# Layer 1's feed-forward block: raw weights loaded in halves, one low part moved to VectorE, down weights and saved operands asked for at other places

## The chip, the cores and the metric

The kernel runs on one core of a Trainium2 chip. The core has a matrix engine (TensorE, PE in the rows), a vector engine (VectorE, DVE), a scalar engine (ScalarE, ACT), GpSimd (POOL) and a sync engine (SyncE, SP) that here only issues DMAs. The metric is the device time of one execution in microseconds (us), the median of several.

## The reference

Two transformer layers on 1024 tokens of width 1024. Every layer ends with `x = x + g1 * o`, a normalisation, and a SwiGLU feed-forward block (D_FF is 2816 = 22 x 128):

```python
def _swiglu(h, wg, wu, wd):
    return (jax.nn.silu(h @ wg) * (h @ wu)) @ wd
...
        x = x + g1 * o
        h = _rms(x, norm2_g[i]) * (1.0 + sc2) + sh2
        x = x + g2 * _swiglu(h, ffn_w_gate[i], ffn_w_up[i], ffn_w_down[i])
```

The change touches only layer 1 after its attention: the output projection and the feed-forward block, the last 865 us or so of the span.

## The kernel before

All products are made in two parts: a matrix is split into a high part (ScalarE casts it) and a low part (the matrix less its high part), and each product is three matmuls (`mm3`, L74 to L76: high by high, low by high, high by low). TensorE, ScalarE, VectorE and GpSimd each run their own instructions in the order in which a list scheduler set them in this part of the program; SyncE issues its DMAs in program order, and each waits there until the buffer it fills is free.

**Output projection** (`out_proj1`). For each of two column halves of the tokens, ci = 0 and 1, it runs over 8 row tiles dt of x. One row tile is 24 matmuls of 128x512 (`d_ps`) and an update of x by VectorE (L1264). In between it advances two generators of normalisation steps (`norm1s`): `own` for the half in work, and `side`. own0 normalises half 0 and ends in four calls of `combine`, which form the operands `c_hi` and `c_lo` of the products (GpSimd sums `s_sum`, ScalarE casts, VectorE low parts). own1 normalises half 1 and stores its result in DRAM (`h_d`).

**Gate and up** (`gate_up1`). For each of 22 tiles f of D_FF and each half ci, the four products of h's two halves with the gate and up weights are made by a scheme of seven products in place of eight (Winograd's form of Strassen's), each 12 matmuls of 128x256 into a tile `p_ps`: 84 matmuls for a tile. The weight operands are four 128x512 blocks, b11 and b21 (the first and second half of the gate tile), b12 and b22 (of the up tile), and four sums by GpSimd: t1 = b12 - b11 (L1325), t2 = b22 - t1 (L1326), t3 = b22 - b12 (L1341), t4 = t2 - b21 (L1345). The order of the products is b11, t2, t3, t1, t4, b21, b22. The split of an operand is `parts_of`: ScalarE casts the high part (L1239). For the first five operands ScalarE also copies the high part to PSUM (`pmisc`, L1243), and VectorE subtracts (L1244). For b21 and b22 GpSimd subtracts (also L1244). High and low parts live in a ring of six buffers. The raw weights, `w_raw`, live in four buffers of 512 KB, two for a tile, so the load of tile f+2 waits for the last reader of tile f.

**Down** (`down1`). After every second tile the products of two tiles with the down weights are made: 8 row tiles of 6 matmuls of 128x512, 48 in all, into `d_ps`; the last two pairs of a half come together. `down_weights1` loads the down weights of a tile (256 KB each by GpSimd's queue, L1381), casts them (ScalarE, L1382) and makes the low parts (GpSimd, L1383). The parts lie in the two tiles of `h_out[1]` (`h_hi` for even pairs, `h_lo` for odd pairs).

**Between the halves**, the saved operands of half 1 are loaded from `h_d` (`h_in`, L1429) into the same four raw buffers, and `combine` is called at row tiles 1 and 5 of each of the last two `down1` of half 0 (`amid`).

Of the kernel before, what the change touches and what calls it, by code (L numbers as in the profile page):

```python
# [9 lines left out]
F32 = mybir.dt.float32  # L10
F32R = mybir.dt.float32r
AF = mybir.ActivationFunctionType
ALU = mybir.AluOpType
# [3 lines left out]
P = 128  # L17
D = 1024
KT = D // P
SEQ = 1024  # L20
# [3 lines left out]
GW = 64  # L24
GH = SEQ // GW
HD = 64
DFF = 2816
NF = DFF // P
# [35 lines left out]
def build(tc, io):  # L64
    nc = tc.nc
    V, S, G, TE = nc.vector, nc.scalar, nc.gpsimd, nc.tensor
# [45 lines left out]
    def vec(l, which):  # L112
        return mod[l][:, which * KT:(which + 1) * KT, :]
# [1113 lines left out]
    ph, ph_cm = pools.open("ph1", bufs=2, psum=True)  # L1227
    HT = 256

    def raw_weights(src):  # L1230
        raw = wr.tile([P, KT, P], F32, name="w_raw")
        nc.sync.dma_start(raw, src)
        return raw

    def parts_of(src, eng=V, past=True):


        hi, lo = (ww.tile([P, 4, P], F32R, name=n) for n in ("w_hi", "w_lo"))
        S.copy(hi, src)  # L1239
        first = fl(hi)  # L1240
        if eng is V and past:
            first = ph.tile([P, 512], F32, name="pmisc").rearrange("p (k n) -> p k n", n=P)
            S.copy(first, fl(hi))  # L1243
        eng.tensor_tensor(lo, src, first, ALU.subtract)  # L1244
        return hi, lo

    def out_weights(dt):
        raw = raw_weights(io["w_out1"][dt])
        old = wr.tile([P, SEQ], F32, name="x_old", tag="w_raw")
        nc.sync.dma_start(old, x_d[:, dt])  # L1250
        return [parts_of(raw[:, i:i + 4], past=False) for i in (0, 4)], old

    def out_proj1(ci, ready, own, side=iter(()), then=lambda: None):

        h_hi, h_lo = h_out[ci]
        for dt in reversed(range(KT)):
# [7 lines left out]
            V.scalar_tensor_tensor(x[:, dt, ci * 512:ci * 512 + 512].rearrange("p (c r) -> p c r", r=GH),  # L1264
                                   ps.rearrange("p (c r) -> p c r", r=GH), vec(1, 2)[:, dt, 0:1],
                                   old.rearrange("p (r c) -> p r c", c=GW)[:, :, cols].rearrange("p r c -> p c r"),
                                   ALU.mult, ALU.add)
# [55 lines left out]
    def first_sums(g, u):  # L1323
        t1, t2 = (wk.tile([P, 4, P], F32, name=n, tag="t", bufs=4) for n in ("t1", "t2"))
        G.tensor_tensor(t1, u[:, 0:4], g[:, 0:4], ALU.subtract)  # L1325
        G.tensor_tensor(t2, u[:, 4:8], t1, ALU.subtract)  # L1326
        return t1, t2

    def gate_up1(f, side=iter(()), raws=None):
        g, u = raws[:2] if raws else load_gate_up(f)  # L1330
        b11, b21, b12, b22 = g[:, 0:4], g[:, 4:8], u[:, 0:4], u[:, 4:8]
        t1, t2 = raws[2:] if raws else first_sums(g, u)
# [6 lines left out]
        S.copy(p1, ps)  # L1339
        w = parts_of(t2)  # L1340
        G.tensor_tensor(t3, b22, b12, ALU.subtract)  # L1341
        ps = product7(w, 4)
        V.tensor_tensor(u2, ps, p1, ALU.add)
        w = parts_of(t3)
        G.tensor_tensor(t4, t2, b21, ALU.subtract)  # L1345
        ps = product7(w, 5)
        V.tensor_tensor(u3, ps, u2, ALU.add)  # L1347
        w = parts_of(t1)
        ps = product7(w, 3)
        V.tensor_tensor(av[:, 1], ps, u3, ALU.add)  # L1350
        V.tensor_tensor(u2, ps, u2, ALU.add)
# [7 lines left out]
        V.tensor_tensor(sg, ps, p1, ALU.add)  # L1359
# [46 lines left out]
    c_lo = cc.tile([P, 7, 4, HT], F32R, name="c_lo")  # L1406
    own1 = norm1s(1, V, keep)
    def first_tile():
        g, u = load_gate_up(0)
        return g, u, *first_sums(g, u)  # L1410

    ready = out_proj1(1, ready, own1, own0, then=first_tile)
    advance(own0, 99)
    for ci in range(2):
        acts = {}
        for f in range(NF):
            if f < NF - 1:
                down_weights1(f + 1 if f else 0)
            if f == 0:
                down_weights1(1)  # L1420
            acts[f] = gate_up1(f, own1 if f else iter(()), ready if f + ci == 0 else None)
            if f % 2 == 0 and 2 <= f < NF - 2:
                down1(ci, (f - 2, f - 1), [acts.pop(f - 2), acts.pop(f - 1)], False)

        h_in = []
        for i in range(4 if ci == 0 else 0):
            h_in.append(wr.tile([P, 2, 512], F32, name="h_in", tag="w_raw"))
            for n in range(2):
                nc.sync.dma_start(h_in[i][:, n], h_d[:, i + 4 * n])  # L1429

        def amid(dt):
            if dt % 4 == 1 and h_in:
                h = h_in.pop(0)
                combine(3 - len(h_in), h[:, 0], h[:, 1], tags=("t", "t"))

        for f in (NF - 4, NF - 2):
            down1(ci, (f, f + 1), [acts.pop(f), acts.pop(f + 1)], f == NF - 2, amid)
    pools.close(ph_cm, pp_cm, pd_cm, wk_cm, ww_cm, wr_cm, xp_cm, cc_cm, bg_cms[1], cst_cm)


# [110 lines left out]
```

## Time and profile before

| what | us |
|---|---|
| median of 3 runs | 2966.08 (2962.96 to 2969.83) |
| profiled execution: its own time | 2964.59 |
| its span | 2962.5 |
| TensorE busy in the span | 2820.2 |
| gate/up and down of half 0, in the span | about 2194 to 2592 |
| gate/up and down of half 1 | to 2958.7 |

The span is cut into stretches below, named by their start and end in us from the span's start. In a view by stretches each row gives the stretch, its length, the busy time and count of each engine's instructions (PE, PEld, DVE, ACT, POOL), the mean clock granted to TensorE as a share of full speed, the busy share of the DMA engines, and GB/s. In a timeline a row is start, length, engine, line, operation, tile written and tiles read, and in brackets how long the engine was idle before and what ended that.

### The profile page before, as it was taken

Reading aid. Unit: us, or ns where it says so; the run is one execution under the profiler, and the core shown is the slowest. Engines: PE = TensorE matmul, PEld = TensorE weight load, DVE = VectorE, ACT = ScalarE, POOL = GpSimd, SP = SyncE. Lnnn points to the kernel's source line nnn. Section 1 sums busy time; section 2 is a strip of 40 time slices with the busy share of each in tenths; the row PEclk is TensorE's granted clock in tenths of the full one; section 3 lists DMA queues with packets and bytes.
Section 4 is the critical chain, followed back from the end, with each engine's and each line's share of the span. In section 5 each row is a group of like instructions: output and inputs, shape, how many; then the busy total and the mean of one; then the engine's idle time right before and its main releaser. Section 6 shows DMA issues by size and latency. Waiting matters only on the chain. (4 is left out here: it accounts for less than half of the span.)

```text
span 2962.5 us, 44248 instructions
## 1 busy us (share of the span) xinstructions
PE 2820.2 (95%) x16874; PEld 2361.8 (80%) x16874; DVE 1555.9 (53%) x3084; ACT 1196.2 (40%) x2358; POOL 847.3 (29%) x914
## 2 busy tenths in 40 slices
PE   7989999999999999999989999999988999889999
PEld 5876768888888888888867888777767888788888
DVE  5775553623323333333575241666477766766666
ACT  4345552511121111111253231666356666565563
POOL 1112332000000000000220001655257666677764
PEclk9989999999999999999999999999989999999999
DMA  7236564211011010111134335975443333332331
GB/s 275 89 113 235 211 213 139 64 43 36 29 50 43 29 43 30 42 43 37 50 107 133 104 104 151 206 167 119 156 144 114 104 97 97 111 120 86 104 97 58
DMA packets 132069, 310.58 MB, mean 105 GB/s; under 512 B 11505, under 2 KB 69361, under 8 KB 124817
## 3 DMA queue, kind: packets, MB, share of 16 engines
q1 hardware_dynamic: 116384, 265.72, 28.7%
q0 software_dynamic: 8992, 31.40, 3.3%
q10 hardware_dynamic: 6480, 10.63, 1.0%
q8 instruction: 133, 2.18, 0.3%
q14 instruction: 80, 0.65, 0.1%
HBM read 264.58 MB, written 43.12 MB: 104 GB/s over the span
## 5 line engine op out<-in xcount | busy, mean ns | idle before, releaser
L76 PE MATMUL p_ps<-c_hi,w_lo 128*128 128x256 f32 x1232 | 352.3, 286 | 39.1 <-POOL w_lo L1244 31.6
L74 PE MATMUL p_ps<-c_hi,w_hi 128*128 128x256 f32 x1232 | 350.7, 285 | 22.2 <-DVE u L1347 5.6
L75 PE MATMUL p_ps<-c_lo,w_hi 128*128 128x256 f32 x1232 | 349.4, 284 | 0.0
L810 POOL TENSOR_TENSOR nrm_ss<-nrm_ss,nrm_sq 128x512 f32<-128x512 f32 (+1 forms) x31 | 39.3, 1268 | 1013.3 <-PE d_ps L76 935.7
L775 ACT CAST w_hi<-w_raw 128x1024 fp32r<-128x1024 f32 x106 | 110.2, 1049 | 481.0 <-PE d_ps L75 270.5
L76 PEld LDWEIGHTS p_ps<-c_hi,w_lo 128*128 128x128 f32 x1232 | 239.7, 195 | 45.6 <-POOL w_lo L1244 37.1
L74 PEld LDWEIGHTS p_ps<-c_hi,w_hi 128*128 128x128 f32 x1232 | 239.8, 195 | 25.2 <-DVE u L1347 5.8
L75 PEld LDWEIGHTS p_ps<-c_lo,w_hi 128*128 128x128 f32 x1232 | 239.9, 195 | 0.9
L580 POOL TENSOR_SCALAR pr<-pr,st 128x640 f32<-128x640 f32 (+2 forms) x208 | 156.0, 750 | 267.8 <-DVE st L579 177.2
L878 DVE SCALAR_TENSOR_TENSOR x<-d_ps,mod,x 128x512 f32<-128x512 f32 (+1 forms) x240 | 157.6, 661 | 125.3 <-PE d_ps L76 125.3
L776 DVE TENSOR_TENSOR w_lo<-w_raw,w_hi 128x1024 fp32r<-128x1024 f32 x102 | 124.2, 1224 | 183.1 <-ACT w_hi L775 180.7
L862 DVE TENSOR_TENSOR sg<-sg,u_ps 128x512 f32<-128x512 f32 (+1 forms) x66 | 39.5, 599 | 320.2 <-PE u_ps L76 320.2
L74 PE MATMUL d_ps<-act_hi,w_hi 128*128 128x512 f32 (+1 forms) x528 | 189.5, 360 | 3.4 <-DVE x L878 3.4
L75 PE MATMUL d_ps<-act_lo,w_hi 128*128 128x512 f32 (+1 forms) x528 | 189.4, 359 | 1.3 <-DVE act_lo L864 1.3
L76 PE MATMUL d_ps<-act_hi,w_lo 128*128 128x512 f32 (+1 forms) x528 | 189.5, 359 | 0.0
L75 PE MATMUL u_ps<-o_lo,w_hi 128*128 128x512 f32 (+1 forms) x528 | 188.6, 357 | 0.0
L76 PE MATMUL u_ps<-o_hi,w_lo 128*128 128x512 f32 (+1 forms) x528 | 188.6, 357 | 0.0
L74 PE MATMUL u_ps<-o_hi,w_hi 128*128 128x512 f32 (+1 forms) x528 | 188.6, 357 | 0.0
L76 PE MATMUL g_ps<-o_hi,w_lo 128*128 128x512 f32 (+1 forms) x528 | 188.5, 357 | 0.0
L74 PE MATMUL g_ps<-o_hi,w_hi 128*128 128x512 f32 (+1 forms) x528 | 188.5, 357 | 0.0
L75 PE MATMUL g_ps<-o_lo,w_hi 128*128 128x512 f32 (+1 forms) x528 | 188.5, 357 | 0.0
L574 ACT ACTIVATE pr<-sm,st 128x640 f32<-128x640 f32 (+4 forms) x208 | 162.7, 782 | 31.0 <-POOL sm L563 22.2
(323 smaller groups left out, 7464.5 us busy)
## 6 DMA issues: line engine op xcount, KB each, us to landing
ada_w<-ada_w SPq DMA_DIRECT2D x48, 1024.0 KB, 4.9
w_raw<-w_gate SPq DMA_DIRECT2D x66, 512.0 KB, 3.5
w_raw<-w_up SPq DMA_DIRECT2D x66, 512.0 KB, 3.6
wd_raw<-w_down POOLq DMA_DIRECT2D x88, 256.0 KB, 2.9
k<-k_d SPq DMA_DIRECT2D x28, 640.0 KB, 10.3
w_raw<-w_out SPq DMA_DIRECT2D x32, 512.0 KB, 3.6
w_raw<-w_in SPq DMA_DIRECT2D x24, 512.0 KB, 4.1
w_raw<-w_down SPq DMA_DIRECT2D x22, 512.0 KB, 3.5
```

What stands on the lines that cost most here:

```text
L74: TE.matmul(out, lh, rh, start=first, stop=False)
L75: TE.matmul(out, lh, rl, start=False, stop=False)
L76: TE.matmul(out, ll, rh, start=False, stop=last)
L574: S.activation(self.pr[:, :n], self.sm[:, :n], AF.Exp, bias=st[:, 0:1], scale=-1.0, accum_out=st[:, 1:2])
L580: G.tensor_scalar(self.pr[:, :n], self.pr[:, :n], st[:, 3:4], 0.0, ALU.mult, ALU.add)
L775: S.copy(hi, raw)
L776: eng.tensor_tensor(lo, raw, fl(hi), ALU.subtract)
L810: adder(i).tensor_tensor(ss, ss, sq, ALU.add)
L862: V.tensor_tensor(sg[:, :n], sg[:, :n], u_ps[:, :n], ALU.mult)
L878: V.scalar_tensor_tensor(xs, self.shaped(ps[:, :n]), vec(l, 5)[:, dt, v:v + 1], xs, ALU.mult, ALU.add)
```

## The change

`w_raw` becomes eight buffers of 256 KB. A tile is loaded by four DMAs in the order b11, b12, b22, b21 in place of two. The output projection's weights and its old x come in halves through the same buffers, and the update of x is two instructions for 8 of 16 rows each in place of one. The low part of b21 is made by VectorE, with a copy of its high part to PSUM by ScalarE. `side` is advanced by 3 steps for a row tile in place of 2. `down_weights1(f)` is called after `gate_up1(f)`; before, tile f+1's call came ahead of `gate_up1(f)`. The first of the four pairs of saved operands is loaded into two work tiles (tags `nrm_ss` and `nrm_r`), the other three pairs into six half buffers, and `combine` is called at row tiles 3 and 7 of the first of the last two `down1` and at 1 and 4 of the second. Nothing of the arithmetic changes but which engine makes one subtraction. In the changed file the lines named above stand one to three lines lower (L1239 is L1240, L1244 is L1245, L1325 is L1328, L1381 is L1383, L1383 is L1385).

```diff
-    wr, wr_cm = pools.open("raw1", bufs=4)
+    wr, wr_cm = pools.open("raw1", bufs=8)
...
-    def raw_weights(src):
-        raw = wr.tile([P, KT, P], F32, name="w_raw")
-        nc.sync.dma_start(raw, src)
-        return raw
+    def raw_half(src):
+        raw = wr.tile([P, 512], F32, name="w_raw")
+        dst = raw if len(src.shape) == 2 else raw.rearrange("p (k n) -> p k n", n=P)
+        nc.sync.dma_start(dst, src)
+        return dst
...
     def out_weights(dt):
-        raw = raw_weights(io["w_out1"][dt])
-        old = wr.tile([P, SEQ], F32, name="x_old", tag="w_raw")
-        nc.sync.dma_start(old, x_d[:, dt])
-        return [parts_of(raw[:, i:i + 4], past=False) for i in (0, 4)], old
+        ws = [parts_of(raw_half(io["w_out1"][dt][:, i:i + 4]), past=False) for i in (0, 4)]
+        return ws, [raw_half(x_d[:, dt, i:i + 512]) for i in (0, 512)]
...
-            V.scalar_tensor_tensor(x[:, dt, ci * 512:ci * 512 + 512].rearrange("p (c r) -> p c r", r=GH),
...
+            for i in range(2):
+                rows = slice(8 * i, 8 * i + 8)
+                V.scalar_tensor_tensor(
...
             advance(own, 1)
-            advance(side, 2)
+            advance(side, 3)
...
     def load_gate_up(f):
-        return [raw_weights(io[w][1, f]) for w in ("w_gate", "w_up")]
+
+        return [raw_half(io[w][1, f][:, i:i + 4]) for w, i in (("w_gate", 0), ("w_up", 0), ("w_up", 4), ("w_gate", 4))]
...
-        w = parts_of(b21, G)
+        w = parts_of(b21)
...
         for f in range(NF):
-            if f < NF - 1:
-                down_weights1(f + 1 if f else 0)
-            if f == 0:
-                down_weights1(1)
             acts[f] = gate_up1(f, own1 if f else iter(()), ready if f + ci == 0 else None)
+            down_weights1(f)
             if f % 2 == 0 and 2 <= f < NF - 2:
                 down1(ci, (f - 2, f - 1), [acts.pop(f - 2), acts.pop(f - 1)], False)
 
         h_in = []
         for i in range(4 if ci == 0 else 0):
-            h_in.append(wr.tile([P, 2, 512], F32, name="h_in", tag="w_raw"))
-            for n in range(2):
-                nc.sync.dma_start(h_in[i][:, n], h_d[:, i + 4 * n])
-
-        def amid(dt):
-            if dt % 4 == 1 and h_in:
-                h = h_in.pop(0)
-                combine(3 - len(h_in), h[:, 0], h[:, 1], tags=("t", "t"))
+            if i:
+                h_in.append([raw_half(h_d[:, k]) for k in (i, i + 4)])
+            else:
+                h_in.append([wk.tile([P, 512], F32, name="h_in", tag=t) for t in ("nrm_ss", "nrm_r")])
+                for h, k in zip(h_in[0], (0, 4)):
+                    nc.sync.dma_start(h, h_d[:, k])
+
+        def amid(i):
+            if h_in and i in (3, 7, 9, 12):
+                combine(4 - len(h_in), *h_in.pop(0), tags=("t", "t"))
```

**How the order moves.** GpSimd in the steady part, where a row's names are `w_lo` (a low part written), `w_hi` (its high part) and `w_raw` (a raw block; the numbers tell one buffer's use from another). Before, from the low part of tile 11's b22 to that of tile 12's b22:

```order
L1244 TENSOR_TENSOR w_lo_21198<-w_raw_21058,w_hi_21197 128x512
L1325 TENSOR_TENSOR t1_21464<-w_raw_21462,w_raw_21460 128x512
L1326 TENSOR_TENSOR t2_21465<-w_raw_21462,t1_21464 128x512
L1341 TENSOR_TENSOR t3_21468<-w_raw_21462 128x512
L1345 TENSOR_TENSOR t4_21469<-t2_21465,w_raw_21460 128x512
L1244 TENSOR_TENSOR w_lo_21348<-w_raw_21226,w_hi_21347 128x512
L1244 TENSOR_TENSOR w_lo_21368<-w_raw_21228,w_hi_21367 128x512
```

Changed, the same place in the loop (here from tile 9 to tile 10):

```order
L1245 TENSOR_TENSOR w_lo_20918<-w_raw_20774,w_hi_20917 128x512
L1328 TENSOR_TENSOR t1_21194<-w_raw_21188,w_raw_21186 128x512
L1329 TENSOR_TENSOR t2_21195<-w_raw_21190,t1_21194 128x512
L1343 TENSOR_TENSOR t3_21198<-w_raw_21190,w_raw_21188 128x512
L1347 TENSOR_TENSOR t4_21199<-t2_21195,w_raw_21192 128x512
L1245 TENSOR_TENSOR w_lo_21094<-w_raw_20950,w_hi_21093 128x512
```

The low part of b21 has left GpSimd's list; t1 now reads two blocks (b12, b11) that are not the block (b22, now 20774 and 21190) whose buffer the first row sets free.

SyncE's list between the halves. Before, from tile 21's two loads to tile 0's of the second half:

```order
L1232 DMA w_raw_23004<-w_gate 128x1024
L1232 DMA w_raw_23006<-w_up 128x1024
L1429 DMA h_in_23166<-h_d_18025 128x512 x2
L1429 DMA h_in_23169<-h_d_18025 128x512 x2
L1429 DMA h_in_23172<-h_d_18025 128x512 x2
L1429 DMA h_in_23175<-h_d_18025 128x512 x2
L1232 DMA w_raw_23386<-w_gate 128x1024
```

Changed:

```order
L1233 DMA w_raw_23202<-w_gate 128x512
L1233 DMA w_raw_23204<-w_up 128x512
L1233 DMA w_raw_23206<-w_up 128x512
L1233 DMA w_raw_23208<-w_gate 128x512
L1233 DMA w_raw_23382<-h_d_18025 128x512
L1233 DMA w_raw_23384<-h_d_18025 128x512
L1233 DMA w_raw_23386<-h_d_18025 128x512
L1233 DMA w_raw_23388<-h_d_18025 128x512
L1233 DMA w_raw_23390<-h_d_18025 128x512
L1233 DMA w_raw_23392<-h_d_18025 128x512
L1233 DMA w_raw_23586<-w_gate 128x512
```

Six half loads of the saved operands stand here in place of eight; the other two have moved up into the loads of the first half's earlier tiles.

More of the change, by code (lines that the diff above doesn't have):

```diff
@@ L1263, in out_proj1 @@
             cols = slice(ci * 32, ci * 32 + 32)
-            V.scalar_tensor_tensor(x[:, dt, ci * 512:ci * 512 + 512].rearrange("p (c r) -> p c r", r=GH),
-                                   ps.rearrange("p (c r) -> p c r", r=GH), vec(1, 2)[:, dt, 0:1],
-                                   old.rearrange("p (r c) -> p r c", c=GW)[:, :, cols].rearrange("p r c -> p c r"),
-                                   ALU.mult, ALU.add)
+            for i in range(2):
+                rows = slice(8 * i, 8 * i + 8)
+                V.scalar_tensor_tensor(
+                    x[:, dt, ci * 512:ci * 512 + 512].rearrange("p (c r) -> p c r", r=GH)[:, :, rows],
+                    ps.rearrange("p (c r) -> p c r", r=GH)[:, :, rows], vec(1, 2)[:, dt, 0:1],
+                    old[i].rearrange("p (r c) -> p r c", c=GW)[:, :, cols].rearrange("p r c -> p c r"),
+                    ALU.mult, ALU.add)
             advance(own, 1)
-            advance(side, 2)
+            advance(side, 3)
         return ready
@@ L1320, in load_gate_up, with first_sums @@
     def load_gate_up(f):
-        return [raw_weights(io[w][1, f]) for w in ("w_gate", "w_up")]
-    def first_sums(g, u):
+        return [raw_half(io[w][1, f][:, i:i + 4]) for w, i in (("w_gate", 0), ("w_up", 0), ("w_up", 4), ("w_gate", 4))]
+    def first_sums(b11, b12, b22):
         t1, t2 = (wk.tile([P, 4, P], F32, name=n, tag="t", bufs=4) for n in ("t1", "t2"))
-        G.tensor_tensor(t1, u[:, 0:4], g[:, 0:4], ALU.subtract)
-        G.tensor_tensor(t2, u[:, 4:8], t1, ALU.subtract)
+        G.tensor_tensor(t1, b12, b11, ALU.subtract)
+        G.tensor_tensor(t2, b22, t1, ALU.subtract)
         return t1, t2
     def gate_up1(f, side=iter(()), raws=None):
-        g, u = raws[:2] if raws else load_gate_up(f)
-        b11, b21, b12, b22 = g[:, 0:4], g[:, 4:8], u[:, 0:4], u[:, 4:8]
-        t1, t2 = raws[2:] if raws else first_sums(g, u)
+        b11, b12, b22, b21 = raws[:4] if raws else load_gate_up(f)
+        t1, t2 = raws[4:] if raws else first_sums(b11, b12, b22)
         t3, t4 = (wk.tile([P, 4, P], F32, name=n, tag="t", bufs=4) for n in ("t3", "t4"))
@@ L1408, in first_tile @@
     def first_tile():
-        g, u = load_gate_up(0)
-        return g, u, *first_sums(g, u)
+        raws = load_gate_up(0)
+        return *raws, *first_sums(*raws[:3])
     ready = out_proj1(1, ready, own1, own0, then=first_tile)
```

3 lines of the change are left out of this document (2 added, 1 removed).

## The prediction

> **What bounds the kernel now.** I read first how long each stretch of the feed-forward block takes, from the view by stretches (columns: length, then busy time and count of PE, PEld, DVE, ACT, POOL, granted clock, DMA share, GB/s).
>
> ```profile
> 2190.21:2254.04 63.83, 49.00 (x317) 44.64 (x316) 46.53 (x69) 45.30 (x83) 49.03 (x46) 0.87 0.34 118
> 2254.04:2331.52 77.48, 65.31 (x433) 59.23 (x432) 57.05 (x83) 42.85 (x80) 54.96 (x48) 0.96 0.37 119
> 2331.52:2549.56 218.04, 207.02 (x1465) 191.88 (x1464) 142.09 (x255) 135.54 (x247) 151.46 (x132) 0.98 0.30 96
> 2549.56:2642.88 93.32, 78.67 (x483) 69.46 (x481) 63.94 (x103) 49.70 (x96) 68.45 (x64) 0.95 0.38 126
> 2642.88:2907.12 264.24, 249.94 (x1729) 230.33 (x1728) 173.73 (x304) 158.68 (x289) 182.47 (x159) 0.98 0.30 95
> 2907.12:2958.70 51.58, 51.57 (x349) 46.65 (x347) 32.62 (x56) 19.88 (x38) 16.25 (x13) 1.00 0.14 51
> ```
>
> Then what TensorE needs if nothing stalls it: one tile's 84 products and one down, in the same view cut to their own matmuls.
>
> ```profile
> 2293.89:2303.42 9.53, 9.53 (x84) 9.53 (x84) 2.01 (x5) 0.37 (x1) 1.00 0.19 57
> 2417.49:2428.68 11.19, 11.19 (x48) 8.86 (x48) 5.25 (x7) 0.00 (x0) 1.00 0.20 62
> ```
>
> A pair of tiles and its down thus need 2 x 9.53 + 11.19 = 30.25. Against this the stretches lose: the start (three tiles, one down, and 17 last matmuls of the output projection at some 0.23, an estimate from that stage's rate) 63.83 - 39.8 - 3.9 = 20.1; the next four tiles with two downs, beside which the second half's normalisation runs, 77.48 - 60.5 = 17.0; half 0's steady part (14 tiles, 6 downs) 218.04 - 200.6 = 17.4; the passage between the halves (4 tiles, 144 matmuls of down) 93.32 - 71.7 = 21.6; half 1's steady part (8 pairs) 264.24 - 242.0 = 22.2; the end 51.58 - 51.0 = 0.6. Together 99, and nothing else of the program is touched except the output projection.
>
> The steady loss is one loop between two engines and a queue. TensorE waits there for one thing only (waits in 2642.88 to 2907.12; total us, times, longest):
>
> ```profile
> PE p_ps L76 <- POOL w_lo L1244: 14.3, 10, 2.0
> POOL t L1325 <- DMA w_raw<-w_up: 70.6, 16, 5.7
> ```
>
> and GpSimd's timeline shows why, with SyncE's issues under it:
>
> ```profile
> 2433.84 1.31 POOL L1383 TENSOR_TENSOR h_lo<-wd_raw,h_lo 128x512 fp32r<-128x512 f32 x1
> 2435.45 0.55 POOL L1381 DMA_DIRECT2D wd_raw<-w_down  x1 [0.30 <-POOL h_lo L1383]
> 2436.02 1.31 POOL L1244 TENSOR_TENSOR w_lo<-w_raw,w_hi 128x512 fp32r<-128x512 f32 x1
> 2441.78 1.30 POOL L1325 TENSOR_TENSOR t<-w_raw 128x512 f32<-128x512 f32 x1 [4.45 <-DMA w_raw<-w_up]
> 2443.16 1.29 POOL L1326 TENSOR_TENSOR t<-w_raw,t 128x512 f32<-128x512 f32 x1
> 2444.41 1.30 POOL L1341 TENSOR_TENSOR t<-w_raw 128x512 f32<-128x512 f32 x1
> 2445.67 1.26 POOL L1345 TENSOR_TENSOR t<-t,w_raw 128x512 f32<-128x512 f32 x1
> 2446.90 2.51 POOL L1244 TENSOR_TENSOR w_lo<-w_raw,w_hi 128x512 fp32r<-128x512 f32 x2
> 2454.23 1.30 POOL L1325 TENSOR_TENSOR t<-w_raw 128x512 f32<-128x512 f32 x1 [4.82 <-DMA w_raw<-w_up]
> ...
> 2437.36 0.33 SPq L1232 DMA_DIRECT2D w_raw<-w_up  x1
> 2448.19 0.33 SPq L1232 DMA_DIRECT2D w_raw<-w_gate  x1
> 2449.44 0.33 SPq L1232 DMA_DIRECT2D w_raw<-w_up  x1
> ```
>
> The low part of b22 of tile f (2436.02) ends at 2437.33; at 2437.36 the load of tile f+2's up weights leaves; GpSimd stands 4.45 until it has landed, makes t1 to t4, and only then the low parts of b21 and b22 of tile f+1 (the double row). Its next b22 is done 12.1 later (2449.41 less 2437.33). Where no down lies between, TensorE wants it after 9.53. In the other interval of a pair four down low parts with their four issues stand in the same list, 4 x (1.31 + 0.55 + 0.30) = 8.6, so 20.7 against TensorE's 9.53 + 11.19 = 20.7: no room to make it up. Per pair 12.1 - 9.5 = 2.6 is lost; the rows say (264.24 - 242.0) / 8 = 2.8.
>
> **The change part by part.**
>
> *The loop.* One subtraction leaves GpSimd's list, and t1 (b12 - b11) no longer reads the block that comes last. From one b22 low part to the next GpSimd then has: wait for b22 of tile f+2 (t1's 1.3 lies inside it), t2, t3, t4 and the low part, 4 x 1.25 = 5.0 by the starts above. What a 256 KB load by SyncE in this loop takes no row shows. The issue rows have both sizes (KB each, median us to landing):
>
> ```profile
> w_raw<-w_gate SPq DMA_DIRECT2D x39, 512.0 KB, 3.5
> wd_raw<-w_down POOLq DMA_DIRECT2D x78, 256.0 KB, 2.9
> ```
>
> So 2.9 at best and, with nothing gained by the smaller size, the 4.45 of now: 7.9 to 9.5 in the short interval, against 9.53; with 8.6 more, 16.5 to 18.1 in the long one, against 20.7. At both ends GpSimd is done in time, so the value does not hang on it. t4 also needs b21, issued behind b22, but two sums (2.5) lie before it. The loads of b11 and b12 wait for early readers only. I price the pair at 30.25 plus 0.1, an allowance: saved 39.6 - 1.5 = 38. At no gain in the loop it is 0.
>
> The slow clock in this sum goes with the waits. Of the 22.2 of half 1, 14.3 is waiting and 249.94 - 242.0 = 7.9 longer busy time, at a granted 0.98; the last stretch, which waits for nothing, has 1.00 and loses 0.6.
>
> *The added work.* Each tile gets one more copy on ScalarE and one more subtraction on VectorE; the costs are those of (busy us, mean ns):
>
> ```profile
> L1243 ACT COPY pmisc<-w_hi 128x512 f32<-128x512 f32 x80 | 47.3, 591 | 2.5
> L1244 DVE TENSOR_TENSOR w_lo<-w_raw,pmisc 128x512 fp32r<-128x512 f32 x16 | 11.0, 687 | 8.8 <-ACT pmisc L1243 8.8
> ```
>
> 44 x (0.59 + 0.69) = 56 of work, which I set at nothing on the path. By the stretch of half 1, VectorE had 173.73 / 8 = 21.7 for a pair and gets 23.1 of 30.25; ScalarE had 19.8 and gets 21.0. The cover is the ring of six operands, refilled while the down runs. It is thin inside two tiles in a row: less the down's 5.25, VectorE has (23.1 - 5.25) / 2 = 8.9 for 9.53. That ScalarE is ahead is seen in its waiting for TensorE to free the ring:
>
> ```profile
> ACT w_hi L1239 <- PE p_ps L75: 23.4, 38, 1.8
> ```
>
> If the cover fails, up to 56 comes back: a rival.
>
> *Passage between the halves.* The saved operands are asked for late: SyncE's row shows the eight loads as one group 14 long, the buffers freed one by one by GpSimd's low parts, and ScalarE, then VectorE behind it, stand for them. Later ScalarE stands for down weights:
>
> ```profile
> 2546.92 13.96 SPq L1429 DMA_DIRECT2D h_in<-h_d  x8
> ...
> 2560.88 0.40 ACT L1311 CAST c_hi<-h_in 128x256 fp32r<-128x256 f32 x1 [7.59 <-DMA h_in<-h_d]
> 2592.25 0.62 ACT L1382 CAST h_lo<-wd_raw 128x512 fp32r<-128x512 f32 x1 [4.68 <-DMA wd_raw<-w_down]
> ...
> PE p_ps L74 <- DVE u L1347: 5.6, 1, 5.6
> PE p_ps L74 <- DVE u L1351: 2.9, 1, 2.9
> ```
>
> In the new order one pair comes tiles earlier, and `combine` sits, counted over the sixteen row tiles, at 3, 7, 9 and 12 in place of 1, 5, 9 and 13. A row tile is 11.19 / 8 = 1.4, so the first two calls stand 2.8 later in the lists, behind loads that leave earlier. Bounds: 0, and 17 of the 21.6, since the combines' own work stays. I take 10: the two waits on u are 8.5, and some slow clock goes with them.
>
> *Half 1's normalisation zone* (17.0). ScalarE's cast of a down weight stands in its list ahead of operand casts, and its load had only been issued:
>
> ```profile
> 2265.37 1.24 ACT L1382 CAST h_hi<-wd_raw 128x512 fp32r<-128x512 f32 x2 [5.71 <-DMA wd_raw<-w_down]
> ...
> PE p_ps L74 <- DVE sg L1359: 4.2, 1, 4.2
> PE p_ps L74 <- ACT p L1339: 3.3, 1, 3.3
> PE d_ps L74 <- DVE x L1392: 4.7, 4, 1.7
> ```
>
> Asked for after the tile's products, these casts stand behind the operands. Queued behind them are only the next tile's casts, with the ring between. Bounds 0 (they wait elsewhere) and 13; I take 8: the first wait, 4.2, goes and takes slow clock along in proportion (17.0 / 12.2 x 4.2 = 5.9); of the other waits, 8.0, I add a quarter, a choice between none and all.
>
> *The start* (20.1). TensorE waits for t2's cast and a low part that stands behind half 0's last combine:
>
> ```profile
> 2195.55 0.62 ACT L1239 CAST w_hi<-t 128x512 fp32r<-128x512 f32 x1 [2.87 <-POOL t L1326]
> 2198.93 2.60 DVE L1312 TENSOR_TENSOR c_lo<-s_sum,c_hi 128x512 fp32r<-128x512 f32 x1
> ```
>
> Three steps of `side` for a row tile finish the combines earlier, but the same work presses into the output projection's 16 row tiles, and each x update there is two instructions: 16 times one fixed cost more, at most 16 x 0.15 = 2.4 (0.69 for 512 columns less two halves at 0.42, rows of the same engine). Bounds -3 and 12; I take 5.
>
> *Sum.* 38 + 10 + 8 + 5 = 61. The profiled execution took 2964.59 (2962.5 is its span), so 2903.6. The median of the runs shown is 1.5 above it: 2905.
>
> **What the Trainium skill says against it.** "DMA: Bandwidth & Descriptors", Rules for kernel authors, wants small transfers coalesced, at 1 MiB or more. By its section on the anatomy of a DMA (2.0 plus bytes / 436e3) a half would take 2.6 and a whole 3.2, an estimate from that page, so that halves cost fixed time but land sooner. The rows of this case agree in kind (2.9 and 3.5); by the rule alone the loop would still close in 2.6 + 5.0 = 7.6.
>
> **The rivals.**
>
> *The slow clock stays.* TensorE's lost clock could be no matter of these waits: then the 7.9 of half 1 and 207.02 - 200.6 = 6.4 of half 0 remain, 14 less saved: 2919. For it: the waits are short (2.0 at most). Against: the waitless end at 1.00. "TensorE: Matmul & The Clock Gate", What's actually happening, ties half speed to an idle window of about 3.4, longer than any wait of the loop; the trace, with 0.98 beside waits of 2 and 1.00 beside none, speaks for a shorter one. Chance 0.07.
>
> *Only the loop pays.* The three other zones keep their waits in another place (VectorE is busy 46.5 of 63.8 in the start and 57.1 of 77.5 in the next): 2966 - 38 = 2928. Chance 0.17.
>
> *The ends give more:* 16, 12 and 12 of the zones' 17, 13 and 12: 2966 - 38 - 40 = 2888. It needs the combines wholly out of the way. Chance 0.10.
>
> *VectorE and ScalarE become the bound*, also the way in which the change would not do what it says: t1's wait goes, and TensorE waits for `pmisc` and VectorE's low parts instead. With all 56 on the path, 2905 + 56 = 2961, no change. Against it: 23.1 of 30.25. Chance 0.03.
>
> *Slower: the queue.* If loads of one queue were served one after another, a tile's four halves and its two down loads would take 6 x 2.9 = 17.4, more than the (264.24 / 16) = 16.5 that a tile takes now. It decides once the sum passes 16.5; the price is 0.9 x 44 = 39, so 3005. Against: two loads issued at 2448.19 and 2449.44 had both landed by 2454.23, where one after another they need 3.5 + 3.5 = 7.0, until 2455.2; and DMA is busy at 0.30. Chance 0.04.
>
> **How the numbers follow.** My forecast, 2905 (own range 2892 to 2920), has 0.59. The range reaches from 2882, which takes in the case of better ends, to 2936, past the loop-only case; outside are the last two rivals and some margin of all. This kernel's measurement tells about 0.2% (6) from no change: faster holds all but the last two, 0.93; same 0.03; slower 0.04.
>
> **What would show it.** Right: GpSimd's wait before t1 is gone, and a shorter one (2 to 4) stands before t2, L1329; no wait of TensorE for GpSimd's low part; pairs at 30.3 to 30.5, and the clock at 1.00 in both steady parts; one GpSimd low part for a tile. Wrong: TensorE waiting for VectorE's low part of b21 or for ScalarE's casts in the tile after another; a wait of over 4.5 before t2; in the passage, waits on u as long as now; in the start, VectorE's updates of x late for TensorE's `d_ps`.

## The result and the profile after

The changed kernel takes 2947.9 us (median of 4 runs, 2942.7 to 2949.2) against 2968.0 before: a ratio of 0.993 (95% interval 0.991 to 0.995), 20 us faster. The forecast was 61. The profiled execution has a span of 2947.4, 15.1 less than before.

The view by stretches of the changed kernel, cut at the same tiles as before (length, busy time and count of PE, PEld, DVE, ACT, POOL, granted clock, DMA share, GB/s):

```profile
2204.35:2261.27 56.92, 47.72 (x318) 43.42 (x317) 41.21 (x73) 43.93 (x80) 34.35 (x28) 0.88 0.34 117
2261.27:2341.25 79.98, 67.59 (x434) 60.30 (x433) 59.82 (x89) 46.35 (x89) 54.65 (x52) 0.91 0.41 135
2341.25:2550.38 209.13, 202.05 (x1466) 187.05 (x1464) 156.04 (x267) 141.18 (x258) 137.60 (x121) 1.00 0.31 102
2550.38:2638.52 88.14, 76.55 (x483) 67.16 (x481) 71.70 (x110) 52.47 (x102) 60.69 (x59) 0.98 0.36 125
2638.52:2892.48 253.96, 244.43 (x1730) 224.20 (x1728) 189.34 (x320) 166.93 (x305) 163.95 (x143) 1.00 0.30 99
2892.48:2943.60 51.12, 51.12 (x349) 46.44 (x347) 32.90 (x58) 21.14 (x40) 11.68 (x9) 1.00 0.08 32
```

Read against the rows of before, in us (minus is saved):

| part | before | changed | difference | forecast |
|---|---|---|---|---|
| up to the first matmul of the output projection | 2097.4 | 2102.6 | +5.2 | 0 |
| output projection and tiles 0 to 2 of half 0 | 156.6 | 158.7 | +2.1 | -5 |
| tiles 3 to 6 (normalisation zone) | 77.5 | 80.0 | +2.5 | -8 |
| half 0 steady | 218.0 | 209.1 | -8.9 | -38 with half 1 |
| passage between the halves | 93.3 | 88.1 | -5.2 | -10 |
| half 1 steady | 264.2 | 254.0 | -10.3 | |
| end | 51.6 | 51.1 | -0.5 | 0 |

The first part is code that the change does not touch; in the profiles of this study it ends anywhere from 2096.4 to 2103.4, for kernels with the same code there. The profiled execution of the changed kernel is thus 5 worse there than that of before, and the sum of the parts below it, -20.3, is close to what the medians show; two profiles of one kernel (act_lo to GpSimd, below) differ there by 4.8 as well.

In the steady part the wait that bounded the kernel is gone, and another stands there. The waits of TensorE and of GpSimd in half 1's steady part (total us, times, longest):

```profile
PE d_ps L74 <- DVE x L1394: 9.5, 8, 1.3
POOL t L1328 <- DVE w_lo L1245: 21.1, 16, 1.9
```

No wait for GpSimd's low part, none of GpSimd for a load. A half has landed in 2.6 to 2.7 after its issue (KB each, median us), where a whole of before took 3.5 (gate) or 3.9 (up):

```profile
w_raw<-w_gate SPq DMA_DIRECT2D x78, 256.0 KB, 2.6
w_raw<-w_up SPq DMA_DIRECT2D x78, 256.0 KB, 2.7
```

In its place TensorE waits once in every pair for VectorE's first updates of x, which free the three `d_ps` buffers. VectorE's timeline at a down that starts at 2752.81 shows what stands ahead of them:

```profile
2754.91 1.34 DVE L1366 TENSOR_TENSOR av<-u,sg 128x256 f32<-128x256 f32 x1
2756.17 0.68 DVE L1245 TENSOR_TENSOR w_lo<-w_raw,pmisc 128x512 fp32r<-128x512 f32 x1
2756.93 0.69 DVE L1369 TENSOR_TENSOR act_lo<-av,act_hi 128x512 fp32r<-128x512 f32 x1
2757.54 2.06 DVE L1394 SCALAR_TENSOR_TENSOR x<-d_ps,mod,x 128x512 f32<-128x512 f32 x3
```

Three row tiles of the down take 3 x 1.4 = 4.2; the fourth needs the first buffer back, at 2757.0. The first update starts at 2757.54, 4.7 after the down's start (1.6 in the kernel before), takes 0.75 and so ends 1.3 too late; TensorE waits 1.2. The second row is the low part that the change gave to VectorE (b21 of the next tile). A pair takes 31.75 (253.96 / 8) for 33.03 before and 30.25 of pure work.

In tiles 3 to 6 the two long waits are for updates of x too, 3.7 and 7.1. The waits of TensorE there, then VectorE, GpSimd and TensorE around the longer one:

```profile
PE d_ps L74 <- DVE x L1394: 10.8, 2, 7.1
PE p_ps L74 <- DVE sg L1361: 0.8, 1, 0.8
...
2324.09 0.74 DVE L1394 SCALAR_TENSOR_TENSOR x<-d_ps,mod,x 128x512 f32<-128x512 f32 x1
2324.75 0.67 DVE L1245 TENSOR_TENSOR w_lo<-t,pmisc 128x512 fp32r<-128x512 f32 x1
2325.34 7.60 DVE L1369 TENSOR_TENSOR act_lo<-av,act_hi 128x512 fp32r<-128x512 f32 x1
2332.87 1.40 DVE L1394 SCALAR_TENSOR_TENSOR x<-d_ps,mod,x 128x512 f32<-128x512 f32 x2
...
2324.40 1.30 POOL L1329 TENSOR_TENSOR t<-w_raw,t 128x512 f32<-128x512 f32 x1
2325.65 1.28 POOL L1343 TENSOR_TENSOR t<-w_raw 128x512 f32<-128x512 f32 x1
2326.90 1.26 POOL L1347 TENSOR_TENSOR t<-t,w_raw 128x512 f32<-128x512 f32 x1
2328.12 1.25 POOL L1385 TENSOR_TENSOR h_lo<-wd_raw,h_lo 128x512 fp32r<-128x512 f32 x1
2329.32 0.56 POOL L1383 DMA_DIRECT2D wd_raw<-w_down  x1
2329.90 1.27 POOL L1385 TENSOR_TENSOR h_lo<-wd_raw,h_lo 128x512 fp32r<-128x512 f32 x1
2331.12 1.27 POOL L1385 TENSOR_TENSOR h_hi<-wd_raw,h_hi 128x512 fp32r<-128x512 f32 x1
2332.33 1.62 POOL L1383 DMA_DIRECT2D wd_raw<-w_down  x3
...
2333.66 0.79 PE L74 MATMUL d_ps<-act_hi,h_hi 128*128 128x512 f32 x1 [7.12 <-DVE x L1394]
```

One subtraction of VectorE, 0.69 in the median, lasts 7.60: as long as GpSimd computes one thing after another, with one DMA issue between, and TensorE stands 7.12 behind it.

### The profile page after: what moved, and what is told of

It reads as the page before. It is cut to its first block, busy times and chain, and to the rows that moved or that the text cites. A ratio compares the mean times of both kernels' runs of the same rounds, so it can differ in the third digit from the quotient of the medians.

```text
span 2947.4 us, 44547 instructions
## 1 busy us (share of the span) xinstructions
PE 2812.9 (95%) x16874; PEld 2350.1 (80%) x16874; DVE 1592.2 (54%) x3144; ACT 1219.9 (41%) x2402; POOL 799.0 (27%) x870
## 5 line engine op out<-in xcount | busy, mean ns | idle before, releaser
L74 PE MATMUL p_ps<-c_hi,w_hi 128*128 128x256 f32 x1232 | 344.6, 280 | 13.6 <-ACT w_hi L1240 4.6
L76 PE MATMUL p_ps<-c_hi,w_lo 128*128 128x256 f32 x1232 | 343.0, 279 | 4.5 <-DVE w_lo L1245 3.5
L75 PE MATMUL p_ps<-c_lo,w_hi 128*128 128x256 f32 x1232 | 342.7, 278 | 0.0
L74 PEld LDWEIGHTS p_ps<-c_hi,w_hi 128*128 128x128 f32 x1232 | 233.7, 190 | 17.5 <-ACT w_hi L1240 6.6
L76 PEld LDWEIGHTS p_ps<-c_hi,w_lo 128*128 128x128 f32 x1232 | 233.5, 190 | 5.8 <-DVE w_lo L1245 4.5
L75 PEld LDWEIGHTS p_ps<-c_lo,w_hi 128*128 128x128 f32 x1232 | 233.6, 190 | 0.9
## 6 DMA issues: line engine op xcount, KB each, us to landing
k<-k_d SPq DMA_DIRECT2D x28, 640.0 KB, 10.5
```

The source lines that it names most:

```text
L74: TE.matmul(out, lh, rh, start=first, stop=False)
L75: TE.matmul(out, lh, rl, start=False, stop=False)
L76: TE.matmul(out, ll, rh, start=False, stop=last)
```

## The experiments

Each is timed against the kernel before, 3 rounds; the ratio is given with its 95% interval. "Pair" is half 1's steady part over 8.

**b21's low part back to GpSimd**, all else as changed.

```diff
-        w = parts_of(b21)
+        w = parts_of(b21, G)
```

> The changed kernel with b21's low part back on GpSimd (no extra copy on ScalarE, no extra subtraction on VectorE); halves, eight buffers and all else as changed. Theory (VectorE's list): each steady pair of the changed kernel loses 1.42 because the first updates of x after a down stand on VectorE behind the extra low part and act_lo; without the extra one TensorE's waits on x in the steady part go, pairs come to 30.3 to 30.5 in place of 31.67, and 15 pairs give some 19 us: about 2929 (2922 to 2936). Rival (the loop of load and GpSimd closes again with two low parts for a tile): GpSimd needs 2.7 + 0.3 for the load, 3.75 for t2 to t4 and 2.6 for two low parts, 9.35, or 10.7 if the load takes 4; then TensorE waits for GpSimd's low part again, pairs 31.5 to 33: 2945 to 2965.

Measured: 2930.5, ratio 0.988 (0.986 to 0.989). TensorE has no wait in half 1's steady part, and a pair takes 30.6 (its row by stretches, then VectorE at a down that starts at 2769.41):

```profile
2627.80:2872.80 245.00, 244.67 (x1730) 223.49 (x1729) 184.04 (x304) 157.21 (x289) 187.31 (x159) 1.00 0.30 102
...
2771.51 1.35 DVE L1366 TENSOR_TENSOR av<-u,sg 128x256 f32<-128x256 f32 x1
2772.77 0.74 DVE L1394 SCALAR_TENSOR_TENSOR x<-d_ps,mod,x 128x512 f32<-128x512 f32 x1
```

The first update now starts 3.4 after the down's start in place of 4.7, with neither the extra low part nor act_lo ahead of it. The gain on the kernel before is 35.4 in place of 20.1, so this part of the change costs some 15 here. By the profiles half 1's steady part gives 9.0 of it and tiles 3 to 6, at 73.1, give 6.9; half 0's steady part gives 1.1 only (208.1), and the passage takes 3.7 more (91.9). The time of the theory was thus met with luck: it had counted on fifteen pairs.

**Only b21's low part to VectorE**, in the kernel before.

```diff
-        w = parts_of(b21, G)
+        w = parts_of(b21)
```

> The kernel before with only b21's low part moved to VectorE. Theory (both the loop and VectorE's list bind, the later one counts): GpSimd's short interval falls by one low part, 12.1 to about 10.8, against TensorE's 9.53, so a pair still loses about 1.3 to it; VectorE's wait of about 1.4 lies in the other interval and is not hidden, so pairs at 31.6 to 32.9 and the time 2945 to 2965. Rival 1 (the halves bring all that was gained): pairs as before, 33.0, time 2968. Rival 2 (moving b21 brings all): pairs 31.67 as in the changed kernel, 2949.

Measured: 2934.4, ratio 0.989 (0.988 to 0.991), better than any of the three said; pairs at 31.05. GpSimd still stands for a whole load before t1, but only in some intervals, and TensorE no longer waits for its low part there:

```profile
2628.10:2876.50 248.40, 244.15 (x1729) 224.30 (x1728) 183.18 (x320) 165.67 (x305) 168.92 (x143) 1.00 0.31 101
...
POOL t L1325 <- DMA w_raw<-w_up: 35.5, 9, 4.6
```

My interval of 10.8 against 9.53 was the wrong sum. GpSimd's two intervals of a pair count together, because low parts wait in the ring (a reading of these sums, not timed apart): 12.1 + 20.7 = 32.8 before, which is nearly the pair of 33.03; less two low parts it is 30.3, nothing over TensorE's 30.25.

**The side steps back to 2 for a row tile**, all else as changed.

```diff
-            advance(side, 3)
+            advance(side, 2)
```

> The changed kernel with the side steps of the output projection back at 2 for a row tile. Theory (three steps put a whole combine's chain over four engines into each row tile, 8 to 9 us for TensorE's 5.6): the end of tile 2 of half 0 comes back from 2261.3 to about 2254 to 2257, 4 to 7 us: 2941 to 2944. Rival (the split update of x and the halved loads cost it): the end of tile 2 stays at 2259 to 2262, 2946 to 2949.

Measured: 2945.3, ratio 0.993 (0.991 to 0.995), no difference from the changed kernel that this can tell. From the first matmul of the output projection to the end of tile 2 it takes 156.8, for 158.7 changed and 156.6 before. But the kernel of the next but one experiment, with three steps, takes 156.8 as well. The steps are not shown to matter to this sum, and the 8 to 9 for a row tile that I had put down to them stay unexplained.

**Down weights asked for where they were**, all else as changed.

```diff
+            if f < NF - 1:
+                down_weights1(f + 1 if f else 0)
+            if f == 0:
+                down_weights1(1)
             acts[f] = gate_up1(f, own1 if f else iter(()), ready if f + ci == 0 else None)
-            down_weights1(f)
```

> The changed kernel with the down weights asked for where they were before (tile f+1's ahead of tile f's products). Theory (the new place changes little; what TensorE waits for in tiles 3 to 6 of half 0 is VectorE's updates of x behind the normalisation's steps): the wait of 4 for a down weight's cast comes back in part, tiles 3 to 6 take 78 to 84 (80.0 as changed), time 2946 to 2953. Rival (asking later moved the casts and low parts into VectorE's and ScalarE's busy places and made the waits of 3.9 and 7.3 on x): they go, tiles 3 to 6 take 70 to 74, 2938 to 2943.

Measured: 2931.2, ratio 0.988 (0.986 to 0.990), against the theory and beyond the rival. Tiles 3 to 6 take 67.6 in place of 80.0, the passage 84.2 in place of 88.1; pairs stay as long, 31.67.

```profile
2260.20:2327.80 67.60, 63.05 (x433) 57.03 (x432) 53.78 (x88) 43.87 (x83) 50.07 (x45) 1.00 0.42 141
```

Asking later cost 12 there, together with b21 on VectorE: with b21 on GpSimd the two places give 73.1 (late, the first experiment) and 72.5 (early, below), the same.

**The passage as before**, all else as changed.

```diff
-            if i:
-                h_in.append([raw_half(h_d[:, k]) for k in (i, i + 4)])
-            else:
...
+            h_in.append([raw_half(h_d[:, k]) for k in (i, i + 4)])
...
-            if h_in and i in (3, 7, 9, 12):
+            if h_in and i in (1, 5, 9, 13):
```

> The changed kernel with the passage between the halves as before: all four pairs of saved operands loaded after tile 21's weights, combine at row tiles 1 and 5 of each of the last two downs; the loads stay halves. Theory (the new places bring the 5.2 that the passage gained, 93.3 to 88.1): it goes back to 92 to 94, time 2951 to 2955. Rival (the passage gained from b21's low part leaving GpSimd, as the kernel before with that alone took 86.5 with the old places): 86 to 89, time 2946 to 2949.

Measured: 2942.0, ratio 0.993 (0.991 to 0.994). The gain on the kernel before is 22.1 in place of 20.1. The passage takes 88.3, as changed (88.1), so the new places of the saved operands bring nothing; the passage gained from the rest. The profiled execution is 7.7 shorter than that of the changed kernel, but 3.0 of this lie ahead of the output projection, 1.9 from there to the end of tile 2 and 2.3 in tiles 3 to 6, none where the edit is.

**Two parts undone: b21 on GpSimd and the early down weights** (the first and the fourth diff together).

> The changed kernel with two parts undone: b21's low part on GpSimd and the down weights asked for where they were before. Theory (the losses of the two parts are at different places and add up): steady pairs 30.6 as with the first alone, tiles 3 to 6 of half 0 some 68 and the passage 84 to 88 as with the second alone: 2914 to 2924. Rival (the earlier down weights pay only because VectorE and GpSimd were shifted against each other by b21's move): no better than the first alone, 2928 to 2934.

Measured: 2922.6, ratio 0.986 (0.985 to 0.988). In the range, though not by the terms it named: pairs 30.6 as said, the passage 86.0 (91.9 in the first experiment), but tiles 3 to 6 at 72.5 and not 68, while half 0's steady part is 202.6 against 208.1 of the first experiment.

**Halves alone**: the kernel before, with nothing of the change but the half loads, the eight buffers and the update of x in two.

```diff
-    wr, wr_cm = pools.open("raw1", bufs=4)
+    wr, wr_cm = pools.open("raw1", bufs=8)
...
+        return [raw_half(io[w][1, f][:, i:i + 4]) for w, i in (("w_gate", 0), ("w_up", 0), ("w_up", 4), ("w_gate", 4))]
```

> The kernel before with the raw weights and x in halves and eight buffers, and nothing else of the change. Theory (either part alone closes GpSimd's loop, since the slack of the interval with the down carries over to the short one): steady pairs 30.4 to 30.8, about 32 to 36 less in the two steady parts, the zones around them within 5 of before each: 2928 to 2942. Rival (halves do little without b21 off GpSimd): pairs 32 to 33, 2955 to 2968.

Measured: 2924.0, ratio 0.987 (0.985 to 0.988), twice the whole change's gain and a little more than the theory had. Steady pairs 30.6, passage 86.4, tiles 3 to 6 72.5:

```profile
2330.50:2533.30 202.80, 202.53 (x1466) 186.58 (x1464) 151.86 (x254) 133.31 (x245) 156.43 (x135) 1.00 0.33 106
2619.70:2864.40 244.70, 244.36 (x1729) 223.34 (x1728) 184.14 (x304) 157.17 (x288) 186.98 (x158) 1.00 0.32 103
```

Either part closes the loop by itself. All the other parts, put on top of this one, lose 20. Step by step, with each gain taken against the kernel before in the same timing: halves alone 40.0; with three side steps and the new places of the saved operands 41.4; with the down weights asked for later 35.4; with b21 on VectorE, which is the changed kernel, 20.1. With the last two steps in the other order, b21's move costs 7 (41.4 to 34.7) and the late down weights 15.

**Silu's results in PSUM**, all else as changed, so that the two products for av read one operand from SBUF and one from PSUM.

```diff
-        S.activation(sg, sg, AF.Silu)
+        sp = ph.tile([P, 512], F32, name="pmisc")[:, 0:HT]
+        S.activation(sp, sg, AF.Silu)
...
-        V.tensor_tensor(av[:, 0], u2, sg, ALU.mult)
+        V.tensor_tensor(av[:, 0], u2, sp, ALU.mult)
```

(and the same for u3).

> The changed kernel with the two results of Silu written to PSUM in place of SBUF, so that VectorE's two products for av read one operand from SBUF and one from PSUM; no instruction more or less. Theory (a VectorE operation with two operands in SBUF stands while GpSimd works, 426 ns free of it and 1259 beside it, and this 0.8 delays the updates of x): both products at 0.42 to 0.45, the wait on x falls from 1.2 to about 0.4 for a pair, pairs 30.6 to 30.9, 15 pairs give 11 to 15: 2932 to 2938. Rival (the extra low part and its place in VectorE's list alone cause it): the products get shorter or not, pairs stay at 31.5 to 31.7, 2945 to 2949.

Measured: 2954.3, ratio 0.997 (0.996 to 0.998): slower than the changed kernel. The durations came out as the theory said (groups of VectorE in half 1), and the wait for x is gone from the whole program:

```profile
L1361 DVE TENSOR_TENSOR av<-av,pmisc 128x256 f32<-128x256 f32 x16 | 6.7, 421 | 7.3 <-ACT pmisc L1358 7.3
L1368 DVE TENSOR_TENSOR av<-u,pmisc 128x256 f32<-128x256 f32 x16 | 6.6, 414 | 0.0
...
2646.40:2896.50 250.10, 250.10 (x1730) 224.17 (x1729) 177.07 (x321) 157.25 (x305) 163.10 (x143) 1.00 0.32 100
...
PE p_ps L76 <- POOL w_lo L1245: 16.1, 7, 5.4
```

But the scheduler then set another order: some twenty of a down's 48 matmuls stand among a tile's products, and between 2263 and 2400 (tiles 3 to 9) TensorE waits 16.1 for GpSimd's low part (last row). For the pair this run decides nothing (31.25, under another order); for the durations it does.

**act_lo to GpSimd**, all else as changed.

```diff
-        V.tensor_tensor(lo, avf, fl(hi), ALU.subtract)
+        G.tensor_tensor(lo, avf, fl(hi), ALU.subtract)
```

> The changed kernel with one subtraction moved: the low part of the activations (act_lo) by GpSimd in place of VectorE. Theory (the first update of x waits on VectorE behind the product for av, b21's extra low part and act_lo; in tiles 3 to 6 of half 0 an act_lo of 7.6 beside GpSimd's work holds up x for TensorE): the first update starts about 4.0 after the down's start in place of 4.7, the wait falls from 1.4 to 0.7 to 0.9 for a pair, 15 pairs give 8 to 11; tiles 3 to 6 fall from 80 to 68 to 74; together 2927 to 2936. Rival (VectorE's list does not decide, or GpSimd with one more subtraction for a tile becomes the bound): pairs at 31.6 or more, tiles 3 to 6 at 78 or more, 2945 to 2960.

Measured: 2918.4, ratio 0.983 (0.981 to 0.985); once more, 2918.6, ratio 0.985 (0.983 to 0.986). More than the theory had. Tiles 3 to 6 and half 1's steady part, and VectorE at a down that starts at 2761.45:

```profile
2259.70:2325.00 65.30, 62.16 (x434) 56.65 (x433) 48.59 (x84) 44.98 (x86) 53.13 (x49) 1.00 0.44 146
2618.60:2866.10 247.50, 244.31 (x1729) 224.19 (x1728) 179.26 (x304) 166.54 (x304) 184.09 (x158) 1.00 0.30 101
...
2763.54 1.34 DVE L1366 TENSOR_TENSOR av<-u,sg 128x256 f32<-128x256 f32 x1
2764.81 0.67 DVE L1245 TENSOR_TENSOR w_lo<-w_raw,pmisc 128x512 fp32r<-128x512 f32 x1
2765.40 2.05 DVE L1394 SCALAR_TENSOR_TENSOR x<-d_ps,mod,x 128x512 f32<-128x512 f32 x3
...
PE d_ps L74 <- DVE x L1394: 3.2, 8, 0.4
```

The first update starts 3.95 after the down's start, TensorE waits 0.4 in a pair (last row), a pair takes 30.95, and tiles 3 to 6 give back 14.7: with act_lo off VectorE no VectorE instruction there lasts over 1.7.

> The changed kernel with act_lo by GpSimd once more, beside the one with both: 2914 to 2924 as before, pairs at 30.9, tiles 3 to 6 of half 0 at 65.

**b21 on VectorE only in tiles 0 to 6 of half 0**, with the early down weights.

```diff
-    def gate_up1(f, side=iter(()), raws=None):
+    def gate_up1(f, side=iter(()), raws=None, eng=V):
...
-        w = parts_of(b21)
+        w = parts_of(b21, eng)
...
+            acts[f] = gate_up1(f, own1 if f else iter(()), ready if f + ci == 0 else None, V if ci == 0 and f < 7 else G)
```

> The changed kernel with the down weights asked for where they were before, and b21's low part by VectorE only in tiles 0 to 6 of half 0, by GpSimd in all others. Theory (b21 on VectorE pays where GpSimd is late, beside the second half's normalisation, and costs 1.1 a pair where it is not): tiles 3 to 6 about 68 as with the early down weights alone, steady pairs 30.6, about 4 to 5 less than with both undone: 2915 to 2920. Rival (the 4.8 by which tiles 3 to 6 differed between those two kernels come from the list as a whole): tiles 3 to 6 at 72 to 73, 2921 to 2927.

Measured: 2924.8, ratio 0.986 (0.984 to 0.987), in the rival's time: pairs 30.6, tiles 3 to 6 at 74.2, a little above the rival's 73, with a wait of 4.7 on x behind an act_lo that lasts 6.5. So b21 on VectorE in these tiles does not bring the 67.6 back; that the list as a whole decides there is what remains, and no run tests it by itself.

**b21's low part and act_lo both on GpSimd** (the first diff and that of act_lo), all else as changed.

> The changed kernel with b21's low part and act_lo both by GpSimd. Theory (VectorE's list before the first update of x decides the pair, and GpSimd has room: four low parts, eight sums, four down low parts with their issues and two act_lo are 27 of 30.25): pairs 30.4 to 30.6, tiles 3 to 6 of half 0 at 65 to 73, 2 to 5 less than with act_lo alone: 2912 to 2918. Rival (GpSimd at 27 of 30.25 has no room for the waits of its loop): TensorE waits for GpSimd's low parts, pairs 31 to 33: 2922 to 2950.

Measured: 2913.9, ratio 0.982 (0.981 to 0.984), the best of the study. TensorE waits for nothing in half 1's steady part, and a pair takes 30.32:

```profile
2613.30:2855.90 242.60, 242.57 (x1730) 223.94 (x1729) 169.34 (x288) 157.19 (x289) 206.29 (x175) 1.00 0.32 104
```

GpSimd is busy 206.3 of 242.6 there, the most of all these kernels, and does not bind.

In the four kernels here with the same matmul order, the first update of x starts 3.4 (b21 on GpSimd, with act_lo there or not), 3.95 (act_lo on GpSimd) and 4.7 (changed) after the down's start, and it takes 0.74. Where nothing holds it, the fourth row tile starts at 4.2. The update thus ends 0.1 early, 0.5 late and 1.3 late, and TensorE's waits for a pair are 0, 0.4 and 1.2. Beyond these waits a pair takes 0.3 over 30.25 in three of the kernels and 0.07 with both on GpSimd; what that is, these runs do not say.

## Why the prediction was wrong

The sign was right, the size three times too large (61 against 20), and the time, 2947.9, outside the range of 2882 to 2936. By the table above 19 of what is missing lie in the two steady parts, 10.5 in tiles 3 to 6, 7 in the output projection and the start, and 5 in the passage.

- **The loop: right, and oversolved.** GpSimd's wait for the load went, TensorE's wait for its low part went, and a half lands in 2.6 to 2.7, a little under the lower end I gave. The formula that the prediction took from the Trainium skill is given there ("DMA: Bandwidth & Descriptors", Anatomy of one DMA) for transfers that GpSimd issues: it came out for SyncE's halves (2.6), while SyncE's wholes took 3.5 and 3.9 for its 3.2 and GpSimd's own 256 KB loads 2.9 for its 2.6. The shorter wait before t2 that I named as a sign did not come: in half 1's steady part GpSimd waits 1.3 for a tile before t1, for a low part of VectorE, and not for a load. But I did not ask which of the parts is needed. Halves alone take the pair to 30.6, b21 alone to 31.05. I summed each interval against TensorE's own and missed that the ring carries slack from one to the other, so that the sum of 32.8 for a pair is the measure, as I read it now; by it, taking away two low parts alone leaves 30.3.
- **The added work "which I set at nothing on the path": the step that failed.** It named the ring of six operands as cover. The ring covers the operands, and TensorE has indeed no wait for a low part of VectorE in half 1's steady part. It does not cover what stands behind the extra subtraction in VectorE's list: the first update of x, which has to be done within 4.2 of the down's start, three PSUM buffers. Its cost is the difference between 31.75 and 30.6, 1.1 for a pair, and 15 for the kernel by the first experiment, 7 where the down weights are asked for as before. In half 0's steady part the first experiment hides it: there the late down weights hold the part at 208.1, and with both undone it takes 202.6. The rival with VectorE as the bound, at 0.03, named the engine but the wrong wait, and priced it as all of the work or none.
- **VectorE's length as counted: too short.** I took 8.9 of 9.53 from busy time and read the durations of the page as costs (the 5.25 that I took off for the down has seven of its eight updates; with all eight it is 6.0, and 8.6). The product for av grew from a median of 426 to 1281 in the changed kernel (min/median/max, ns; the kernel before, then the changed one), because GpSimd, freed from its wait, now works at that moment: before, 29 of the program's 44 such products have no GpSimd computation beside them, changed 4, and with halves alone 2:

```profile
L1364 DVE TENSOR_TENSOR av<-u,sg x37: 409/426/1429, 2342.4 to 2936.9; 128x256 f32<-128x256 f32 x37
L1366 DVE TENSOR_TENSOR av<-u,sg x37: 410/1281/1436, 2352.1 to 2921.8; 128x256 f32<-128x256 f32 x37
```

  That 0.85 stands ahead of the first update too. In the first experiment, with neither the low part nor act_lo ahead of the update, the product is as long (1.35) and TensorE does not wait, so it is the sum of the three that decides.
- **Tiles 3 to 6: the forecast of 8 saved became 2.5 lost.** The wait that I put down to a down weight's cast went as said (4.2 before; 0.8 is left for that line), though not by the place alone: with the early down weights it is 0.6 with b21 on VectorE and 4.2 with b21 on GpSimd. The step "asked for after the tile's products, these casts stand behind the operands" did not see that GpSimd's down low parts then stand in one run beside VectorE's act_lo, which is held for 7.6. Moving act_lo gives back 14.7, moving the down weights back 12.4.
- **The passage: 5 of the 10,** and not by the step I priced. With the old places and the changed rest it takes 88.3, with the old places and halves alone 86.4, with b21 alone 86.5, and there ScalarE's wait for the saved operands falls from 9.3 to 1.7, 3.7 and 3.2. So these loads were late because the buffers came free late, and either way of closing the loop answers that. Asking later for the down weights takes some of the gain back: in four kernels that do so (changed, b21 on GpSimd, two side steps, the passage as before) one act_lo in the passage lasts 5.0 to 6.3, and it takes 88.1 to 91.9; in all the other experiments no act_lo there lasts over 1.9, and it takes 83.6 to 86.5.
- **The start: 5 forecast, 2 lost,** out of two opposite moves. Tiles 0 to 2 take 56.9 in place of 63.8, and the output projection 101.8 in place of 92.8. The output projection takes 92.8 and 93.0 in the two kernels with whole loads, 97.5 and 98.1 in the two with halves and two side steps, and 98.4 to 103.5 in all with halves and three. So the halves and the update of x in two cost some 5 there, which I had put at 2.4 at most (an update is 2 x 0.66 for 1.12, 0.2 more and not 0.15). TensorE stands there once for 2.4 to 4.7 for GpSimd's sum of squares (`nrm_ss`) in every kernel with halves and in neither with whole loads; why is not shown.
- **The slow clock: right.** The granted clock is 1.00 in both steady parts, and TensorE's busy time falls by 5.0 (half 0) and 5.5 (half 1), though TensorE still waits up to 1.3 in each pair. In half 1's steady part before, the clock is at 0.50 for 3.4 at a time from 2761.26, 2795.39 and 2860.24, each time within 1.4 of the end of a wait of 1.8 to 2.0. The rival in which it stays is out.
- **The queue of half loads** does not bind: no wait for a load in the changed kernel's steady parts.

What stays open: why the halves lengthen the output projection, what three side steps change against two, why the down weights asked for later hold half 0's steady part when b21 is on GpSimd, and what a pair would take with short products for av in an unchanged order.

## What to carry to other kernels

Before moving an instruction to an engine with room, look at what stands behind it in that engine's list and by when that must be done; here the bound was a release of a PSUM buffer due 4.2 after a stage's start, not the engine's share of busy time. When two edits answer the same wait, time each alone: either closed this loop, halves alone were worth 40 and b21 alone 31, and all parts together 20. And sum a producer's work over the whole period that its ring of buffers spans, not interval by interval.

## What the runs showed of the hardware

VectorE's operations with two operands in SBUF depend on what GpSimd does at that time. Worked out from the instruction times after 2100 us in the changed kernel: the product av<-u,sg takes 426 ns on average in the 4 cases in which no GpSimd computation runs beside it, and 1259 in the 38 in which one runs for over 70% of its length; additions with one operand in PSUM (u<-p_ps,u) take 417 and 415. Written with one operand in PSUM the product took 403 to 422 in all 44 cases. The Trainium skill's "SBUF — State Buffer", Who interferes with whom, says that a VectorE instruction with two SBUF inputs contends with a GpSimd instruction that reads SBUF, while one with a single SBUF input does not: the trace agrees with both. Its Summary: rules for kernel authors has the second to issue blocked until the first finishes; the act_lo of 7.60 above started beside a GpSimd sum that ended at 2325.7 and then outlasted five more GpSimd computations one after another (2325.65 to 2332.4, with one DMA issue of 0.56 between), so the wait was not for one instruction only.
